# Two changes to a two-layer hybrid trunk step: all 16 K tiles of the heads' projection pairs by Strassen, and two of the rotation's six vector operations on GpSimd

## The chip, the core and the metric

The kernel runs on one core of a Trainium2 chip. The core has five engines with a queue of instructions each: TensorE (PE; its weight loads are listed as PEld), VectorE (DVE), ScalarE (ACT), GpSimd (POOL) and SyncE (SP). Each engine takes its queue in order; semaphores tie the queues together. The metric is the device time of one execution in microseconds (us), the median of the runs of a kernel.

## What is computed

The reference is one step of a two-layer trunk on 512 prompt tokens and 8 sample tokens, 520 columns in all, all in fp32. For each layer:

```python
h = rmsnorm(x)
B, C, xc, g_c, q, k, v, g_r = split(h @ w_in)          # 2048 x 8192
y_c = B * conv3(C * xc) * silu(g_c)                     # 1024 wide
q, k = rope(q), rope(k) / 16                            # 4 heads of 256
y_r = groupnorm(retention(q, k, v)) * silu(g_r)
x = x + concat(y_c, y_r) @ w_out
x = x + sigmoid(x @ w_pg) * (p @ w_ple)
```

`rope` takes the two halves `x1, x2` of a head's 256 rows and gives `x1*cos - x2*sin` and `x1*sin + x2*cos`. At the end stands a last norm. The outputs are the tokens and the new states of the convolution and the retention.

## The kernel before

**Layout.** Features lie on the 128 partitions and tokens on the free axis: 2048 features are 16 tiles of 128x520 (the K tiles), and a projection makes output tiles of 128x520. The tokens are worked in two halves of 260 columns, `LEFT` and `RIGHT`.

**Three matmuls for one product.** TensorE works on values rounded to fp32r, so every operand is split into a rounded part `hi` and a rest `lo`. A weight tile is split by `split_w` (line 225): ScalarE writes `hi` (line 229) and VectorE writes `lo` as the raw weights minus `hi` (line 230, two inputs from SBUF). A product of one weight tile (128x128) and one half of a K tile (128x260) is then three matmuls, lines 247, 248 and 249 (`mm3`).

**Pairs.** Output tiles are made in pairs. `plain` (line 270) makes all 2 x 16 x 2 = 64 products of a pair. `strassen` (line 290) takes the first `s` of the 16 K tiles as a 2x2 block scheme: two output tiles, even and odd K tiles, two halves of the tokens. There 7 products stand for 8, at the price of sums of weight tiles (`add`, line 315, VectorE at line 319, two SBUF inputs, four sums of `s/2` tiles a pair) and of sums of operand tiles that are built once for a stage. What is left of the K tiles behind `s` is done plainly in the same accumulators. The seven products of `s/2` tiles are cut by `times` (line 321) into chunks of at most 4 tiles; a chunk is one load into the split ring, one `split_w`, and 4 products, so 12 matmuls:

```python
        def times(out, raw, xs, start, more):
            for i, j in chunks(0, q, CHS):
                w = split_w(raw[:, P * i : P * j])
                product(out, w, 0, xs[i:j], start and i == 0, j == q, more)
                split_ring.put(*w)
```

With `s = 14`, `s/2 = 7`: each of the seven products is a chunk of 3 and a chunk of 4 tiles, and the two K tiles left over make two chunks of 2 tiles (`parts`, line 239), each used for 4 products. With `s = 16` every chunk has 4 tiles and nothing is left over. A pair with `s < 16` holds a fourth accumulator `c` and copies it once more on ScalarE (line 307 by way of `copy`, line 327, written `ps_g<-ps_g` in the profile).

**How many K tiles go by Strassen** stands in tables at the top: `HEADS` (line 53) for the 16 pairs of the four heads in each layer, `CONVS` (line 54) for the 16 pairs of the convolution's branch, and two more for `w_out` and `w_pg`. 0 means `plain`. In `CONVS` 13 of 16 entries are 16. The first two pairs of layer 0 are made apart, before the tables are used.

**The buffers that run ahead.** Raw weights come by SP's queue into a ring of 32 tiles (line 211). Split weights stand in a ring of 60 tiles (line 212): a chunk of 4 takes 8 of them, `hi` and `lo`, and gives them back when its last matmul is done. So ScalarE and VectorE can be up to seven chunks ahead of TensorE, and a wait of `split L229` or `split L230` for a matmul means that this ring is full.

**The heads' stage.** For each head `retain` (line 818) makes the pairs q, k, v and gate. q and k go through `rope` (line 749), six operations of 128x520 on VectorE, lines 753 to 758; `rc` and `rs` are the cosine and sine tables. The results go to memory by GpSimd's DMA queue (line 815, `hs`), and a head's retention is worked in nine later steps that lie between the products of the next pairs. Beside that run the 8 sample tokens' states: loads by GpSimd's queue (lines 771 and 772), VectorE at lines 781 and 785, and a store by GpSimd's queue (line 782). GpSimd itself computes only tiny powers (lines 633, 984, 1383) and fills small tiles; else it issues DMAs.

**What sets the order.** The order of the instructions of each engine is set at build time by a scheduler that estimates when each would be ready; weight splits and weight sums are raised in priority (lines 227 and 318). At run time each engine then follows that order.

Of the kernel before, what the change touches and what calls it, by code (L numbers as in the profile page):

```python
# [11 lines left out]
MUL, ADD, SUB = ALU.mult, ALU.add, ALU.subtract  # L12
# [37 lines left out]
EARLY = 6  # L50


HEADS = [[0, 0, 0, 8] + [14] * 12, [0] + [14] * 15]
CONVS = [[14] * 2 + [16] * 13 + [14]] * 2
OUT_ROWS = [[0, 8, 16, 16, 16, 16, 16, 0]] * 2

# [23 lines left out]
class Slots:  # L80
# [8 lines left out]
    def get(self, dtype=F32):  # L89
        i = self.free.pop(0)  # L90
        self.count += 1
        t = self.pool.tile([P, T], dtype, tag=f"s{i}", name=f"slot{i}_{self.count}")
        self.used[id(t)] = (t, i)
        return t
# [4 lines left out]
    def put(self, *slots):  # L99
        for t in slots:  # L100
            self.free.append(self.used.pop(id(t))[1])
# [90 lines left out]
def trunk_kernel(  # L192
# [6 lines left out]
    V, S, G, PE, DMA = nc.vector, nc.scalar, nc.gpsimd, nc.tensor, nc.sync  # L199
# [363 lines left out]
    def norm_g(l, k):  # L563
        return vec[:, 16 * l + k : 16 * l + k + 1]
# [97 lines left out]
    def from_dram(src):  # L662
        def load(k):
            t = get()
            SIDE.dma_start(t, src[k])
            return t

        return load

    xs = []  # L670
    X = Operands(HEADS[0][2:] + CONVS[0], from_dram(xT), gain=lambda k: norm_g(0, k))
    X.todo = [t for t in ((i, False, True) for i in range(max(X.rows) // 2))]
# [43 lines left out]
    for l in range(DEPTH):  # L716
# [5 lines left out]
        def prepare():  # L722
            rc, rs = get(), get()
            SIDE.dma_start(rc, cosT)
            SIDE.dma_start(rs, sinT)
            with tc.high_priority():
                root = rms.root()
                rb = rms.spread(rms.diagonal(root))
                V.tensor_tensor(rc, rc, rb, MUL)
                V.tensor_tensor(rs, rs, rb, MUL)  # L730
            return root, rb, rc, rs

        def copied(ps):
            t = get()
            for n, v in zip((LEFT, RIGHT), ps):
                S.activation(t[:, n], v, AF.Copy)
            banks.put(*[v for v in ps if not any(v is o for o in over)])
            return Val(put, slot=t)
# [3 lines left out]
        root, rb, rc, rs = prepare()  # L742
# [6 lines left out]
        def rope(z0, z1):  # L749

            a, b = ((z if z.ps is None else copied(z.ps)).slot for z in (z0, z1))
            t1, t2 = get(), get()
            V.tensor_tensor(t1, a, rc, MUL)
            V.tensor_tensor(t2, a, rs, MUL)
            V.tensor_tensor(a, b, rs, MUL)
            V.tensor_tensor(t1, t1, a, SUB)  # L756
            V.tensor_tensor(b, b, rc, MUL)
            V.tensor_tensor(b, b, t2, ADD)
            put(a, t2)
            return [t1, b]  # L760

# [56 lines left out]
        def retain(h):  # L818
# [6 lines left out]
            if l == 0 and h == 0:  # L825
                q = rope(*first[:2])
            else:
                q = rope(*head(mt))
# [5 lines left out]
            if l == 0 and h == 0:  # L834
                kf = rope(*first[2:])
            else:
                kf = rope(*head(mt + 2))
# [335 lines left out]
        if not tail:  # L1173
            X = Operands(HEADS[l + 1] + CONVS[l + 1], next_in, RESERVE_NEXT, gain=lambda k, l=l: norm_g(l + 1, k))
        for m in range(0, KT - tail, 2):
# [303 lines left out]
```

## Time and profile before

| | |
|---|---|
| runs of the kernel before | 2172.50, 2166.74, 2170.08 us; median 2170.08 us |
| profiled execution, own time | 2172.46 us |
| its span in the trace | 2170.4 us |
| busy in the span: PE, PEld | 2148.5, 2142.9 us |
| busy: DVE, ACT, POOL | 1895.7, 1266.2, 430.5 us |
| instructions | 48198, of them 17861 on PE |
| DMA | 387.31 MB, mean 178 GB/s |
| granted TensorE clock, mean | 0.998 |

The profiled execution's own time is 2.4 us above the median of the runs and about equal to the slowest of them. The heads' stages lie at about 60 to 400 us (layer 0) and 1105 to 1460 us (layer 1) of the span, the convolution's at about 400 to 745 and 1460 to 1815 us. A windows view gives the busy time of each engine in such a stretch; a timeline view lists instructions by start and duration; a waits view says who waited for whom, in us in total, times, and the longest; a lines view groups instructions by line and shape with the mean duration in ns of one.

### The profile page before, as it was taken

The page shows a single profiled execution, that of the slowest core. Times are in us where ns is not written, and L with a number is a line of the kernel's source. Part 1 is how long each engine was busy: PE and PEld are TensorE (multiplying, and loading weights), DVE is VectorE, ACT ScalarE, POOL GpSimd, SP SyncE. Part 2 cuts the span into 40 slices and gives each one's busy share as a digit, 9 for nine tenths or more (in the row PEclk, how much of TensorE's full clock was granted, in tenths as well). Part 3 has the DMA queues.
Part 4 walks back from the last instruction along what each step waited for, and adds up shares of the span by engine and source line. Part 5 has one row for each costly group of instructions (what it writes and reads, how often), then busy time and mean ns, then how long its engine had stood idle before and what let it go on. Part 6 is the DMA issues. An engine that isn't in the chain of part 4 may idle for free. (4 is left out here: it accounts for less than half of the span.)

```text
span 2170.4 us, 48198 instructions
## 1 busy us (share of the span) xinstructions
PE 2148.5 (99%) x17861; PEld 2142.9 (99%) x17861; DVE 1895.7 (87%) x3849; ACT 1266.2 (58%) x2661; POOL 430.5 (20%) x746
## 2 busy tenths in 40 slices
PE   9999999999999999999999999999999999999998
PEld 9999999999999999999999999999999999999998
DVE  8889989898999987987897988989999998878884
ACT  8656556655555555655765655565655555456565
POOL 2313222211001211210212222231111022121011
PEclk9999999999999999999999999999999999999999
DMA  8556675545543645645645566665464455566455
GB/s 288 176 169 196 185 215 183 186 152 172 156 134 120 228 156 186 217 153 161 214 144 174 172 210 193 190 195 183 147 182 145 127 155 199 181 212 195 127 169 192
DMA packets 182861, 387.31 MB, mean 178 GB/s; under 512 B 25888, under 2 KB 56352, under 8 KB 182624
## 3 DMA queue, kind: packets, MB, share of 16 engines
q1 hardware_dynamic: 129136, 213.77, 31.8%
q0 software_dynamic: 53056, 169.84, 23.8%
q8 instruction: 140, 2.29, 0.4%
q14 instruction: 97, 0.79, 0.1%
q10 hardware_dynamic: 432, 0.61, 0.1%
HBM read 318.96 MB, written 65.15 MB: 177 GB/s over the span
## 5 line engine op out<-in xcount | busy, mean ns | idle before, releaser
L247 PE MATMUL ps_g<-slot,split 128*128 128x260 f32 x5465 | 1532.3, 284 | 9.7 <-ACT slot L307 3.4
L248 PE MATMUL ps_g<-slot,split 128*128 128x260 f32 x5465 | 1535.1, 283 | 0.3 <-DVE slot L555 0.3
L249 PE MATMUL ps_g<-slot,split 128*128 128x260 f32 x5461 | 1520.5, 283 | 0.5 <-DVE split L230 0.5
L229 ACT ACTIVATE split<-raw 128x512 fp32r<-128x512 f32 (+2 forms) x1347 | 778.2, 596 | 587.6 <-DVE raw L319 205.6
L247 PEld LDWEIGHTS ps_g<-slot,split 128*128 128x128 f32 x5465 | 1024.5, 188 | 12.9 <-ACT slot L307 4.2
L248 PEld LDWEIGHTS ps_g<-slot,split 128*128 128x128 f32 x5465 | 1029.3, 188 | 0.5 <-DVE slot L555 0.5
L249 PEld LDWEIGHTS ps_g<-slot,split 128*128 128x128 f32 x5461 | 1020.3, 188 | 0.8 <-DVE split L230 0.7
L230 DVE TENSOR_TENSOR split<-raw,split 128x512 fp32r<-128x512 f32 (+2 forms) x1346 | 844.1, 647 | 176.5 <-PE ps_g L248 85.4
L319 DVE TENSOR_TENSOR raw<-raw 128x512 f32<-128x512 f32 (+1 forms) x660 | 426.2, 656 | 28.1 <-DMA raw<-wi 18.4
L307 ACT ACTIVATE slot<-ps_g 128x260 f32<-128x260 f32 x336 | 127.2, 381 | 142.5 <-PE ps_g L249 127.2
L551 ACT ACTIVATE slot<-slot 128x520 fp32r<-128x520 f32 (+1 forms) x212 | 109.1, 562 | 41.8 <-DVE slot L414 10.2
L552 DVE TENSOR_TENSOR slot<-slot,slot 128x520 fp32r<-128x520 f32 (+1 forms) x212 | 122.9, 609 | 4.3 <-ACT slot L551 4.2
L782 POOL DMA_DIRECT2D o_rets<-slot x64 | 35.3, 552 | 350.6 <-DVE slot L781 131.8
L307 DVE TENSOR_TENSOR slot<-ps_g,slot 128x260 f32<-128x260 f32 x168 | 70.5, 421 | 7.3 <-PE ps_g L249 4.9
L870 POOL DMA_DIRECT2D slot<-hs x64 | 46.1, 723 | 126.5 <-DVE split L230 35.5
L815 POOL DMA_DIRECT2D hs<-slot x64 | 35.6, 556 | 137.9 <-DVE slot L756 59.6
L747 DVE TENSOR_TENSOR slot<-slot,slot 128x520 f32<-128x520 f32 x80 | 55.4, 692 | 4.6 <-DMA o_rets<-slot 3.7
L1059 POOL DMA_DIRECT2D slot<-x1s x76 | 40.8, 538 | 88.0 <-PE ps_g L249 28.3
L781 DVE SCALAR_TENSOR_TENSOR slot<-slot,vs,slot 128x256 f32<-128x256 f32 x128 | 55.9, 477 | 2.6 <-ACT slot L777 2.3
L1209 POOL DMA_DIRECT2D x2s<-slot x30 | 16.3, 545 | 203.4 <-DVE slot L1204 202.5
L771 POOL DMA_DIRECT2D slot<-sret x64 | 35.5, 555 | 106.4 <-ACT split L229 43.4
L772 POOL DMA_DIRECT2D slot<-kq x64 | 34.9, 547 | 109.2 <-DVE slot L877 20.5
(217 smaller groups left out, 1727.0 us busy)
## 6 DMA issues: line engine op xcount, KB each, us to landing
raw<-wi SPq DMA_DIRECT2D x377, 256.0 KB, 3.9
raw<-wo SPq DMA_DIRECT2D x128, 256.0 KB, 5.6
raw<-wg SPq DMA_DIRECT2D x122, 256.0 KB, 4.2
raw<-wi SPq DMA_DIRECT2D x136, 192.0 KB, 4.0
slot<-x1s POOLq DMA_DIRECT2D x76, 260.0 KB, 5.0
slot<-sret POOLq DMA_DIRECT2D x64, 256.0 KB, 4.0
hs<-slot POOLq DMA_DIRECT2D x64, 256.0 KB, 3.9
slot<-hs POOLq DMA_DIRECT2D x64, 256.0 KB, 5.1
```

Of the source, the lines that this page charges most:

```text
L229: S.activation(hi, raw, AF.Copy)
L230: V.tensor_tensor(lo, raw, F(hi), SUB)
L247: PE.matmul(out, wh, xh, start=start, stop=False, skip_group_check=more)
L248: PE.matmul(out, wh, xl, start=False, stop=False, skip_group_check=more)
L249: PE.matmul(out, wl, xh, start=False, stop=stop, skip_group_check=more)
L307: fn(*args)
L319: V.tensor_tensor(out[:, n], x[:, n], y[:, n], op)
L551: keep(S.activation(hi, src[:, n], AF.Copy))
L552: V.tensor_tensor(lo, src[:, n], F(hi), SUB)
L747: V.tensor_tensor(out[:, n], v, table[:, n], MUL)
L781: keep(V.scalar_tensor_tensor(st[:, c], k, vs[:, h, e, b : b + 1], st[:, c], MUL, ADD))
L870: SIDE.dma_start(t[:, :512].rearrange("p (m n) -> p m n", m=2), src)
```

## The change

Two edits. In `HEADS`, the entries 14 become 16: 12 pairs in layer 0 and 15 in layer 1, 27 in all. The host packs these pairs' weights in the matching order of K tiles by the same table. In `rope`, the product `b * rs` (line 755) and the last sum (line 758) go from VectorE to GpSimd, and the product `b * rc` is written right behind the first of them.

```diff
-HEADS = [[0, 0, 0, 8] + [14] * 12, [0] + [14] * 15]
+HEADS = [[0, 0, 0, 8] + [16] * 12, [0] + [16] * 15]
...
             t1, t2 = get(), get()
             V.tensor_tensor(t1, a, rc, MUL)
             V.tensor_tensor(t2, a, rs, MUL)
-            V.tensor_tensor(a, b, rs, MUL)
+            G.tensor_tensor(a, b, rs, MUL)
+            V.tensor_tensor(b, b, rc, MUL)
             V.tensor_tensor(t1, t1, a, SUB)
-            V.tensor_tensor(b, b, rc, MUL)
-            V.tensor_tensor(b, b, t2, ADD)
+            G.tensor_tensor(b, b, t2, ADD)
             put(a, t2)
             return [t1, b]
```

Line 755 reads `b` and line 756 now overwrites it, so VectorE's line 756 waits for GpSimd's line 755; line 757 needs its result too; and GpSimd's line 755 overwrites `a`, so it waits for VectorE's lines 753 and 754.

SyncE's queue of weight loads shows the first edit. Before, in the heads' stage of layer 0 (`raw` is the ring of raw weights, `wi` the packed `w_in`; 128 columns are one tile):

```order
L312 DMA raw<-wi 128x512
L312 DMA raw<-wi 128x384
L312 DMA raw<-wi 128x512
L312 DMA raw<-wi 128x384
L312 DMA raw<-wi 128x512
L222 DMA raw<-wi 128x256 x2
L312 DMA raw<-wi 128x384
L312 DMA raw<-wi 128x512
L312 DMA raw<-wi 128x384 x2
```

And in the changed kernel, the end of the first stretch of layer 0 and all 12 changed pairs behind it:

```order
L222 DMA raw<-wi 128x512 x9
L312 DMA raw<-wi 128x512 x4
L222 DMA raw<-wi 128x512 x4
L312 DMA raw<-wi 128x512 x96
L312 DMA raw<-wi 128x384 x2
```

The chunks of 3 and 2 tiles are gone there: 12 pairs have 8 loads of 4 tiles each, 96 in a row, and the loads of 3 tiles begin again with the convolution's first pairs.

VectorE's queue at the second head's queries in layer 0, before (`slot_143_1422` is `a`, `slot_144_1423` is `b`, `slot_163_1701` and `slot_164_1702` are `t1` and `t2`, `slot_69_733` and `slot_70_734` the tables):

```order
L755 TENSOR_TENSOR slot_143_1422<-slot_144_1423,slot_70_734 128x520
L230 TENSOR_TENSOR split<-raw,split 128x512
L785 ISA slot_140_1403,osum<-slot_139_1402,slot_140_1403 128x256
L785 ISA osum 128x1
L230 TENSOR_TENSOR split<-raw,split 128x384
L756 TENSOR_TENSOR slot_163_1701<-slot_163_1701,slot_143_1422 128x520
L757 TENSOR_TENSOR slot_144_1423<-slot_144_1423,slot_69_733 128x520
L230 TENSOR_TENSOR split<-raw,split 128x512
L230 TENSOR_TENSOR split<-raw,split 128x256 x2
L758 TENSOR_TENSOR slot_144_1423<-slot_144_1423,slot_164_1702 128x520
```

The same place in the changed kernel (`a` is `slot_151_1441`, `b` is `slot_152_1442`, `t1` and `t2` are `slot_163_1690` and `slot_164_1691`):

```order
L754 TENSOR_TENSOR slot_164_1691<-slot_151_1441,slot_70_734 128x520
L230 TENSOR_TENSOR split<-raw,split 128x512 x3
L785 ISA slot_148_1423,osum<-slot_147_1422,slot_148_1423 128x256
L785 ISA osum 128x1
L230 TENSOR_TENSOR split<-raw,split 128x512
L756 TENSOR_TENSOR slot_152_1442<-slot_152_1442,slot_69_733 128x520
L757 TENSOR_TENSOR slot_163_1690<-slot_163_1690,slot_151_1441 128x520
```

Four splits and one sample operation stand between the last reader of `a` on VectorE (line 754) and line 756, which waits for GpSimd. GpSimd's queue there, in the changed kernel:

```order
L782 DMA o_rets<-slot_147_1422 128x512
L755 TENSOR_TENSOR slot_151_1441<-slot_152_1442,slot_70_734 128x520
L758 TENSOR_TENSOR slot_152_1442<-slot_152_1442,slot_164_1691 128x520
L815 DMA hs<-slot_163_1690 128x512
L815 DMA hs<-slot_152_1442 128x512
L771 DMA slot_174_1915<-sret 128x512
L772 DMA slot_175_1916<-kq 128x512
```

The two operations stand ahead of both `hs` stores and of the next sample's loads. Before, GpSimd's queue had only DMAs in that stretch:

```order
L782 DMA o_rets<-slot_139_1402 128x512
L815 DMA hs<-slot_163_1701 128x512
L771 DMA slot_174_1911<-sret 128x512
L815 DMA hs<-slot_144_1423 128x512
L772 DMA slot_175_1912<-kq 128x512
```

There the first `hs` store (of `t1`) could leave when VectorE's line 756 was done; now both stores wait behind line 758.

## Prediction

> **What bounds the kernel now.** I read the page's first part, then who TensorE waits for, then the stages one by one. The page:
>
> ```profile
> PE 2148.5 (99%) x17861; PEld 2142.9 (99%) x17861; DVE 1895.7 (87%) x3849; ACT 1266.2 (58%) x2661; POOL 430.5 (20%) x746
> ```
>
> TensorE is busy for all but 22 us of the span. A busy PE is not proof of a limit, so I looked at its waits in the waits view. These are the longest three in total; the columns are us, times, longest:
>
> ```profile
> PE ps_g L247 <- ACT slot L307: 3.4, 4, 1.1
> PE ps_g L247 <- ACT ps_g L307: 2.9, 4, 1.1
> PE ps_g L247 <- ACT split L229: 1.9, 1, 1.9
> ```
>
> Next to nothing: TensorE runs through. Now the busy times by stage: the heads' two stages, the convolution's two stages, and two quieter stretches inside the latter. Columns are the stretch, its length, then PE, PEld, DVE, ACT, POOL busy (x instructions), clock, DMA share, GB/s:
>
> ```profile
> 60.00:400.00 340.00, 339.97 (x2837) 339.28 (x2836) 306.05 (x672) 202.46 (x442) 94.04 (x163) 1.00 0.59 188
> 400.00:745.00 345.00, 340.30 (x2822) 339.51 (x2821) 315.92 (x636) 195.88 (x421) 55.80 (x88) 1.00 0.52 161
> 1105.00:1460.00 355.00, 353.00 (x2940) 351.52 (x2939) 311.79 (x682) 206.65 (x461) 90.58 (x154) 1.00 0.58 181
> 1460.00:1815.00 355.00, 352.34 (x2938) 351.38 (x2938) 329.62 (x667) 202.82 (x433) 57.35 (x92) 1.00 0.53 166
> ...
> 500.00:600.00 100.00, 100.00 (x837) 100.00 (x836) 89.93 (x177) 52.76 (x108) 13.19 (x23) 1.00 0.53 161
> 1500.00:1600.00 100.00, 100.00 (x840) 100.00 (x839) 93.06 (x186) 57.72 (x119) 17.76 (x30) 1.00 0.55 169
> ```
>
> The heads lose 0.03 and 2.00 us of TensorE. At full load 837 matmuls take 100 us, 119.5 ns each. VectorE is second: 90% and 88% in the heads. The convolution, most of whose pairs have all 16 K tiles by Strassen already, holds 93.06% of VectorE for 100 us with TensorE full. That is what the heads are to become.
>
> How much VectorE may fall behind is told by the waits on the split ring, first in 60 to 400 us, then in 1105 to 1460 us:
>
> ```profile
> ACT split L229 <- PE ps_g L248: 20.6, 32, 2.2
> ACT split L229 <- PE ps_g L249: 20.5, 36, 1.8
> ...
> ACT split L229 <- PE ps_g L248: 25.4, 34, 2.0
> ACT split L229 <- PE ps_g L249: 13.5, 12, 2.4
> ```
>
> 114 times in 695 us the splitting waits because the ring is full. A chunk of 4 tiles feeds 12 matmuls, 12 x 119.5 ns = 1.43 us, and the ring holds seven, so a full ring is up to 10 us of work in hand. A stall of VectorE of one or two us does not reach TensorE there.
>
> **The change part by part.** *TensorE.* Of a pair, 14 tiles by Strassen are 7 x 7 products and the two left-over tiles 4 x 2, together 57; 16 tiles are 7 x 8 = 56. One product is 3 matmuls, 27 pairs, so 81 matmuls go, all 128x260: 81 x 119.5 ns = **-9.7 us**, all on the path, since TensorE never stops.
>
> *VectorE.* The rows by line and shape (columns: busy us, mean ns of one | idle before it):
>
> ```profile
> L230 DVE TENSOR_TENSOR split<-raw,split 128x512 fp32r<-128x512 f32 x1031 | 690.9, 685 | 152.9 <-PE ps_g L248 81.9 <-ACT split L229 53.8 <-issue 7.2
> L319 DVE TENSOR_TENSOR raw<-raw 128x512 f32<-128x512 f32 x520 | 351.9, 684 | 13.7 <-DMA raw<-wi 6.6 <-DMA raw<-wo 4.6
> L230 DVE TENSOR_TENSOR split<-raw,split 128x384 fp32r<-128x384 f32 x249 | 136.1, 550 | 15.3 <-ACT split L229 8.0 <-PE ps_g L248 3.6 <-ACT slot L551 1.6
> L319 DVE TENSOR_TENSOR raw<-raw 128x384 f32<-128x384 f32 x140 | 76.9, 550 | 14.4 <-DMA raw<-wi 11.8 <-DMA raw<-wg 2.1
> L230 DVE TENSOR_TENSOR split<-raw,split 128x256 fp32r<-128x256 f32 x66 | 27.0, 417 | 8.3 <-ACT split L229 8.1
> L755 DVE TENSOR_TENSOR slot<-slot,slot 128x520 f32<-128x520 f32 x16 | 11.1, 691 | 0.0
> ```
>
> Seven splits a pair grow from 3 to 4 tiles, 189 x (685 - 550) = +25.5 us; two splits of 2 tiles go, 54 x 417 = -22.5 us. Four sums a pair grow by a tile, 108 x (684 - 550) = +14.5 us. The rotation gives up lines 755 and 758, which is as long: 32 x 691 = -22.1 us. Together -4.6 us: the second edit pays for the first. ScalarE has the same splits and 27 copies fewer; at 58% it bounds nothing. The DMAs move the same bytes in fewer, larger loads.
>
> *GpSimd.* 32 operations of 128x520 with two inputs from SBUF. The trace has none of that size. Its rows for fills and for the smallest power with two inputs:
>
> ```profile
> L596 POOL MEMSET half_neg<- 128x32 f32 x1 | 0.1, 121 | 0.0
> L885 POOL MEMSET slot<- 128x128 f32 x8 | 1.8, 225 | 0.0
> L984 POOL TENSOR_TENSOR rstp<-rstd,half_neg 128x2 f32<-128x2 f32 x16 | 14.4, 900 | 20.1 <-DVE rstd L983 20.1
> ```
>
> 96 elements more cost 104 ns, 1.08 ns an element for one stream. 520 elements are 0.1 + 0.56 = 0.7 us if the two inputs and the output flow together, and 0.1 + 3 x 0.56 = 1.8 us one after another. I take 1.2 us, two streams in turn, an estimate from these rows. GpSimd is 20% busy, so its own time matters little. What matters is VectorE beside it. Timelines of both engines at three of GpSimd's powers (columns: start us, duration us):
>
> ```profile
> 673.00 0.69 DVE L319 TENSOR_TENSOR raw<-raw 128x512 f32<-128x512 f32 x1
> 674.76 0.69 DVE L230 TENSOR_TENSOR split<-raw,split 128x512 fp32r<-128x512 f32 x1 [1.07 <-issue]
> ...
> 673.17 5.83 POOL L1383 TENSOR_TENSOR rsn<-va,half_neg 128x32 f32<-128x32 f32 x1 [15.82 <-DVE va L1381]
> ...
> 1434.26 0.68 DVE L319 TENSOR_TENSOR raw<-raw 128x512 f32<-128x512 f32 x1
> 1434.86 0.55 DVE L230 TENSOR_TENSOR split<-raw,split 128x384 fp32r<-128x384 f32 x1
> ...
> 1434.50 1.49 POOL L984 TENSOR_TENSOR rstp<-rstd,half_neg 128x2 f32<-128x2 f32 x1 [1.74 <-DVE rstd L983]
> ...
> 358.39 0.68 DVE L319 TENSOR_TENSOR raw<-raw 128x512 f32<-128x512 f32 x1
> ...
> 358.46 1.19 POOL L984 TENSOR_TENSOR rstp<-rstd,half_neg 128x2 f32<-128x2 f32 x1
> ```
>
> At 673 us VectorE stands still for 1.07 us with nothing in the profile that it waits for, while GpSimd reads. At 1434 and 358 us VectorE runs on and GpSimd's 2-element power, 0.90 us on average, takes 1.49 and 1.19 us. So an operation of each engine with two SBUF inputs holds off the other. A held-off VectorE loses between 0 and 1.8 us per GpSimd operation; I take the whole 1.2 us, since line 756 waits for line 755 anyway. 32 x 1.2 = 38.4 us. The Trainium skill, page "SBUF — State Buffer", section "Who interferes with whom", says that such a pair contend for one read interface, and that whoever starts first holds it for its whole instruction. The trace agrees that one blocks the other; that the block lasts the whole instruction it does not show, 1.07 us of 5.83. By the rule the term stays as I took it; by 1.07 us as the most, it would be 32 x 1.07 = 34.2 us and the share below 94.5%.
>
> VectorE in the heads is then 306.05 + 311.79 - 4.6 + 38.4 = 651.6 us of 695 - 9.7 = 685.3 us, **95.1%**, a little over the 93.06% that a stretch of the convolution holds with TensorE full. Here I choose: 1460 to 1815 us, at 92.9%, lost 2.66 us of TensorE in 355, most of it where the stage ends. Doubled to 685 us that is 5.1, against 2.0 now; half of the difference I give to the heads, **+1.5 us**, bounds -2.0 (today's waits go) and +20 (below).
>
> *The new waits.* VectorE's line 756 waits for GpSimd's 755; behind it stand the splits of the next chunks. GpSimd's queue must be free then. It mostly is: it waits for VectorE at the rotation's stores already, here in layer 1:
>
> ```profile
> POOL hs L815 <- DVE slot L756: 39.8, 8, 17.2
> ```
>
> In the changed order at least two, at 14 of the 16 rotations four or more operations of VectorE stand between lines 754 and 756, so the wait costs it little beyond the blocking already counted. The full ring covers it; without that cover it would be 16 times up to 1.2 us, 19 us. The stores of q and k leave a few us later; they are read again a pair or more later.
>
> The sum: 2172.46 us (the profiled execution) - 9.7 + 1.5 = 2164.3; against the median, 2170.08 - 8.2 = **2161.9 us**.
>
> **The rivals.** *A: the blocking eats half of the gain.* Suppose that VectorE can't be used beyond 95% of the heads, 651 us, before TensorE waits one for one. If a GpSimd operation takes from VectorE as long as the two held-up powers took, (1.49 + 1.19) / 2 = 1.34 us, VectorE's load without blocking, 617.84 - 4.6 = 613.2 us, becomes 613.2 + 32 x 1.34 = 656.1 us, 5.1 us over: -9.7 + 5.1 = -4.6, 2165.5 us, no change that can be told. For it: the 1.07 us block. Against: the ring is full 114 times. The Trainium skill, page "GPSIMD Engine Reference", section 3.1, has GpSimd about 1.96 times slower than VectorE at adding two tensors, which on 691 ns would be an estimate of 1.35 us. No run here shows it yet.
>
> *B: VectorE becomes the bound, slower.* Same mechanism, at the upper bound of 1.8 us: 613.2 + 57.6 = 670.8, 20 us over, -9.7 + 20 = +10, 2180 us. It turns to a loss from (651 + 9.7 - 613.2) / 32 = 1.48 us per operation. For it: at 1434 us each engine held the other off in turn, so that both may lose. Against: VectorE's idle time in the heads, 77 us now, would still not be used up (670.8 of 685).
>
> *C: GpSimd costs VectorE nothing,* as at 358 us, where its operation ran its usual 0.68 us. Then VectorE stays at 613.2 of 685 us, 89.5%, as today, and today's 2.0 us of waits may go too: -11.7, 2158.4 us. Against: the 1.07 us.
>
> **How the numbers follow.** My forecast gets 0.47, C 0.13, A 0.25, B 0.15. About 0.3% (6.5 us) is what a measurement of this kernel can tell from no change. Faster by more is the forecast and C, 0.60; the same is A, 0.25; slower is B, 0.15. The range from 2158 to 2172 us holds the forecast, A and nearly all of C, and leaves out B and the rest.
>
> **What would show it.** Right: 81 matmuls fewer at the same 119.5 ns, TensorE's busy time down by about 9.7 us; lines 755 and 758 on POOL near 1.2 us each; VectorE's waits for POOL at line 756 some us in all; DVE near 95% of the heads' stages counting blocked time. Wrong: TensorE idle by more than some 5 us in the heads, waiting for splits (lines 229 and 230), with GpSimd's operations just before, or GpSimd's operations at 1.8 us and more; then B. A median under 2158 would say C.

## The result, and the profile after

| | before | after |
|---|---|---|
| median of the runs beside each other | 2168.77 us (4 runs) | 2191.09 us (4 runs) |
| profiled execution: span | 2170.4 us | 2184.8 us |

The ratio is 1.0099 [1.0075, 1.0123]: slower by about 22 us where 8 us faster was forecast. The profiled execution of the changed kernel (2186.6 us) is the quickest of its runs, so its trace shows the smaller part of the loss, 14.4 us between the spans.

The page of the changed kernel:

```profile
span 2184.8 us, 47686 instructions
PE 2151.3 (98%) x17780; PEld 2141.4 (98%) x17780; DVE 1924.3 (88%) x3763; ACT 1260.5 (58%) x2580; POOL 497.7 (23%) x778
```

The 81 matmuls are gone, but TensorE's busy time rose by 2.8 us. Idle it was 2170.4 - 2148.5 = 21.9 us before and is 2184.8 - 2151.3 = 33.5 us now. The two heads' stages, in the columns of the windows shown before:

```profile
60.00:400.00 340.00, 331.76 (x2709) 329.04 (x2708) 310.40 (x613) 193.01 (x394) 125.73 (x176) 0.98 0.56 183
...
1105.00:1460.00 355.00, 346.14 (x2843) 343.17 (x2842) 321.98 (x629) 198.12 (x405) 122.99 (x166) 0.99 0.55 177
```

In the same stretches TensorE gets through 128 and 97 matmuls fewer than before, and it idles 17 us of 695 where it idled 2. Whom it waits for (us, times, longest):

```profile
PE ps_g L247 <- ACT slot L307: 13.3, 11, 3.1
PE ps_g L247 <- ACT split L229: 4.8, 5, 1.8
PE ps_g L247 <- ACT ps_g L307: 1.7, 1, 1.7
PE ps_g L249 <- DVE split L230: 1.5, 4, 0.6
```

ScalarE is named in all the long ones, with 58% of its time in use. What ScalarE itself waits for is seen in one of them. The timeline of the changed kernel from 344 to 353 us, GpSimd, VectorE, ScalarE and TensorE in turn (start us, duration us, in brackets the idle time before and its releaser):

```profile
344.80 3.23 POOL L755 TENSOR_TENSOR slot<-slot,slot 128x520 f32<-128x520 f32 x1 [0.78 <-DVE slot L754]
349.88 1.66 POOL L758 TENSOR_TENSOR slot<-slot,slot 128x520 f32<-128x520 f32 x1 [0.98 <-DVE slot L756]
...
346.79 2.38 DVE L230 TENSOR_TENSOR split<-raw,split 128x512 fp32r<-128x512 f32 x2
349.10 0.69 DVE L756 TENSOR_TENSOR slot<-slot,slot 128x520 f32<-128x520 f32 x1
349.71 0.69 DVE L757 TENSOR_TENSOR slot<-slot,slot 128x520 f32<-128x520 f32 x1
350.32 1.50 DVE L785 CUSTOM_DVE_ANT_0 slot<-slot,slot 128x256 f32<-128x256 f32 x1
...
350.43 0.21 ACT L839 ACTIVATE qks<-slot 128x8 f32<-128x8 f32 x1 [1.29 <-DVE slot L757]
351.91 0.94 ACT L307 ACTIVATE slot<-ps_g 128x260 f32<-128x260 f32 x3 [1.27 <-DVE osum L785]
...
352.35 0.59 PE L247 MATMUL ps_g<-slot,split 128*128 128x260 f32 x1 [3.02 <-ACT slot L307]
```

Read it upwards. TensorE stands for 3.02 us until ScalarE has copied an accumulator (line 307). ScalarE is late because line 839, ahead of that copy in its queue, waits 1.29 us for VectorE's line 757, and the copy itself 1.27 us more until VectorE's line 785 is through. VectorE never pauses, but twice it is held off: the two splits at 346.79 take 2.38 us instead of some 1.3, and line 785 takes 1.50 us instead of the 0.41 us that it has elsewhere, each while GpSimd's line 755 or 758 runs. Splits are not what is missing: ScalarE's splits at 345.05 and 346.50 us had themselves waited for a matmul, so the ring of split weights was full shortly before.

After such a wait TensorE is slow for a while longer. Windows of the changed kernel, from just ahead of the wait to behind it, and two more (third column on: PE busy and matmuls; the seventh is the granted clock):

```profile
351.40:358.20 6.80, 5.85 (x27) 5.85 (x28) 5.38 (x12) 3.14 (x8) 4.33 (x9) 0.50 0.71 240
358.20:361.60 3.40, 3.40 (x30) 3.40 (x30) 3.40 (x9) 0.47 (x1) 0.00 (x0) 0.99 0.00 0
252.40:255.80 3.40, 3.40 (x16) 3.19 (x15) 3.40 (x11) 0.13 (x1) 2.67 (x5) 0.51 1.02 277
1327.60:1331.00 3.40, 3.40 (x18) 3.40 (x18) 3.40 (x10) 0.29 (x2) 2.54 (x6) 0.51 0.90 266
1430.00:1433.40 3.40, 3.40 (x18) 3.40 (x17) 3.10 (x8) 1.55 (x3) 2.12 (x4) 0.51 0.71 267
```

At half the clock 16 to 18 matmuls pass in 3.4 us instead of 30. In the four stretches 27 + 16 + 18 + 18 = 79 matmuls keep TensorE busy for 5.85 + 3 x 3.4 = 16.05 us; at 119.5 ns they need 9.4, so 6.6 us are lost. The heads of the kernel before have no such stretch, both their windows show 1.00; that kernel has one in the convolution's stage, behind a wait of 1.95 us (16 matmuls from 729.4 to 732.8 us, 1.5 us lost). The Trainium skill, page "TensorE: Matmul & The Clock Gate", section "Why this matters for your kernels", warns of gaps above about 3 us; here a gap of 3.02 us is followed by the half clock, but so is one of 1.76 us at 250 us, so by these runs the limit is lower than stated or depends on where the gap falls.

The spans add up: -9.7 us of matmuls, +11.6 us of idle time, and +12.5 us inside the busy time (2.8 + 9.7), of which the half clock behind waits is 6.6 - 1.5 = 5.1 and the rest is not told apart here; together +14.4.

### The profile page after: what moved, and what is told of

It is laid out like the page before. It is cut to its first block, busy times and chain, and to the rows that moved or that the text cites. A ratio compares the mean times of both kernels' runs of the same rounds, so it can differ in the third digit from the quotient of the medians.

```text
span 2184.8 us, 47686 instructions
## 1 busy us (share of the span) xinstructions
PE 2151.3 (98%) x17780; PEld 2141.4 (98%) x17780; DVE 1924.3 (88%) x3763; ACT 1260.5 (58%) x2580; POOL 497.7 (23%) x778
## 5 line engine op out<-in xcount | busy, mean ns | idle before, releaser
L247 PE MATMUL ps_g<-slot,split 128*128 128x260 f32 x5434 | 1528.1, 284 | 21.7 <-ACT slot L307 13.3
L229 ACT ACTIVATE split<-raw 128x512 fp32r<-128x512 f32 (+1 forms) x1292 | 779.6, 620 | 592.1 <-DVE raw L319 244.0
L230 DVE TENSOR_TENSOR split<-raw,split 128x512 fp32r<-128x512 f32 (+1 forms) x1292 | 865.9, 688 | 182.2 <-PE ps_g L248 96.2
L319 DVE TENSOR_TENSOR raw<-raw 128x512 f32<-128x512 f32 (+1 forms) x660 | 442.5, 680 | 23.6 <-DMA raw<-wi 17.9
L1141 POOL DMA_DIRECT2D x1s<-slot x32 | 17.4, 545 | 186.6 <-DVE slot L1139 186.6
L785 DVE CUSTOM_DVE_ANT_0 slot<-slot,slot 128x256 f32<-128x256 f32 x128 | 57.2, 447 | 0.0
```

The costliest lines, as they stand in the source:

```text
L229: S.activation(hi, raw, AF.Copy)
L230: V.tensor_tensor(lo, raw, F(hi), SUB)
L247: PE.matmul(out, wh, xh, start=start, stop=False, skip_group_check=more)
L319: V.tensor_tensor(out[:, n], x[:, n], y[:, n], op)
L785: V.tensor_tensor_reduce(k, st[:, c], kb[:, :256], 1.0, 0.0, MUL, ADD, osum[:, e, h, b : b + 1])
```

## The experiments

Three theories stood first. **S**: ScalarE's queue stops at the small copies of queries and keys (lines 830 and 839), which wait for GpSimd's line 758. **V**: VectorE, held off by GpSimd's reads, is too late by itself. **K**: VectorE's own work in the heads is already too much with all 16 tiles. Each run is compared with runs of the kernel before on the same chip, whose median lay between 2168.6 and 2171.1 us.

**Each edit alone.** The first with the table only:

```diff
-HEADS = [[0, 0, 0, 8] + [14] * 12, [0] + [14] * 15]
+HEADS = [[0, 0, 0, 8] + [16] * 12, [0] + [16] * 15]
```

> The first edit alone: 27 pairs with 16 K tiles by Strassen, the rotation as before, all six operations on VectorE. Theory S (ScalarE's queue: its copies for the sample tokens wait for GpSimd's line 758, and the weight splits and accumulator copies behind them come late) and theory V (VectorE held off by GpSimd's reads, 32 x 1.17 us, runs short by itself) both say that the loss comes with GpSimd: 81 x 119.5 ns = 9.7 us less than before plus some 2 us of new waits, 2159 to 2163 us, ratio to before 0.996 to 0.998. Theory K (the sixteenth tile itself overloads VectorE: +17.5 us there in the heads with nothing given back, 92.7% busy) says slower than before, 2175 us and more.

Measured: 2182.63 us, 1.0061 [1.0047, 1.0074], as K expected. The second with 14 tiles and the changed rotation:

```diff
-            V.tensor_tensor(a, b, rs, MUL)
-            V.tensor_tensor(t1, t1, a, SUB)
+            G.tensor_tensor(a, b, rs, MUL)
             V.tensor_tensor(b, b, rc, MUL)
-            V.tensor_tensor(b, b, t2, ADD)
+            V.tensor_tensor(t1, t1, a, SUB)
+            G.tensor_tensor(b, b, t2, ADD)
```

> The second edit alone: 14 K tiles as before, lines 755 and 758 on GpSimd. Theories S and V: the same stalls as in the changed kernel without its 9.7 us of matmuls saved, 2190 to 2200 us, with TensorE waiting for ScalarE's lines 229 and 307 in the heads and its clock granted at half after the longest of these. Theory K: VectorE is relieved of 22 us and pays 37 us for blocking; near before, 2165 to 2175 us.

Measured: 2190.52 us, 1.0100 [1.0087, 1.0113], as S and V expected. Each edit loses by itself, +14 and +22 us, and both together lose +22: they don't add. The heads of the run with 16 tiles alone:

```profile
60.00:400.00 340.00, 331.18 (x2735) 329.00 (x2734) 307.12 (x635) 191.87 (x396) 93.67 (x161) 0.99 0.58 184
...
1105.00:1460.00 355.00, 346.36 (x2876) 343.89 (x2875) 320.77 (x651) 198.15 (x406) 90.29 (x150) 1.00 0.56 178
```

VectorE is busy 90.3% of the time there, less than the 93.06% that the prediction thought safe, and TensorE idles 17.5 us.

**ScalarE freed of the small copies.** The changed kernel with:

```diff
-                S.activation(qks[:, d, :NS], q[d][:, SEQ:T], AF.Copy)
+                G.tensor_copy(qks[:, d, :NS], q[d][:, SEQ:T])
...
-                S.activation(qks[:, 2 + d, :NS], kf[d][:, SEQ:T], AF.Copy)
+                G.tensor_copy(qks[:, 2 + d, :NS], kf[d][:, SEQ:T])
```

> The changed kernel, but the copies of the sample tokens' eight columns of q and k (lines 830 and 839) go from ScalarE to GpSimd, behind line 758 in its own queue, so ScalarE never waits for the rotation. GpSimd's two operations a rotation and their blocking of VectorE stay. Theory S: most of the loss goes, 2160 to 2172 us. Theory V: it stays, 2183 to 2193 us.

Measured: 2189.03 us, 1.0101 [1.0087, 1.0115], no better than the changed kernel. S falls. In the changed kernel ScalarE waited 21.5 us in the heads at these small copies, and in this one not at all; yet TensorE's waits for ScalarE's copies of line 307 stay (12.8 us against 13.3) and those for its splits grow (10.7 us against 4.8).

**GpSimd's reads with nobody waiting for them.** 16 tiles; the rotation is four VectorE operations (the products of line 755 and the sum of line 758 are left out of the results), and GpSimd makes the two operations into a tile that nobody reads:

```diff
             V.tensor_tensor(t2, a, rs, MUL)
-            V.tensor_tensor(a, b, rs, MUL)
-            V.tensor_tensor(t1, t1, a, SUB)
+            G.tensor_tensor(aside_out, t2, rs, MUL)
             V.tensor_tensor(b, b, rc, MUL)
-            V.tensor_tensor(b, b, t2, ADD)
+            V.tensor_tensor(t1, t1, t2, SUB)
+            G.tensor_tensor(aside_out, t1, rs, ADD)
```

> Sixteen K tiles; four operations of the rotation on VectorE as in the changed kernel, and two GpSimd operations of the same size at the same places, whose result goes to a tile that nothing reads. The rotated q and k leave out the terms with b*sin and a*sin in the right places, so the outputs are not the reference's. Blocking of VectorE as in the changed kernel, 32 x 1.1 to 1.2 us; no instruction of VectorE or ScalarE waits for GpSimd's result. Theory V: as slow as the changed kernel, 2183 to 2193 us. Theory S: 2158 to 2166 us.

Measured: 2209.99 us, 1.0189 [1.0176, 1.0202], slower than either theory had it. Then the same without GpSimd's two operations, at 16 and at 14 tiles:

> All 16 tiles by Strassen, and the rotation cut to four VectorE operations (left out: the products of line 755 and the sum of line 758, so the keys and queries are wrong); nothing of it on GpSimd. Against the run with all 16 tiles alone VectorE does 32 x 0.69 = 22 us less in the heads. K (bursts of VectorE's work in the heads starve TensorE, and the longer splits and sums tip it): TensorE's idle time in the heads falls from 20 us to under 6, and the 81 matmuls show: 2157 to 2164 us, ratio 0.995 to 0.998. O (it is not VectorE's work but the 16-tile schedule itself, its chunks and loads): the loss stays, 2176 to 2183 us, ratio 1.003 to 1.006.

> 14 tiles as in the kernel before, and the rotation cut to the same four VectorE operations (left out: lines 755 and 758's work). The kernel before idles TensorE only 2.8 us in the heads, so a lighter VectorE can give no more than that. K: 2165 to 2169 us, ratio 0.998 to 1.000, so that 16 tiles beat 14 by 4 to 10 us once the rotation is light. O: the same time here, but 14 tiles stay 10 us and more ahead of 16.

Measured: 2171.96 us, 1.0004 [0.9993, 1.0014] with 16 tiles; 2172.52 us, 1.0007 [0.9998, 1.0017] with 14. The first lies between the ranges of K and O, the second above both: with 14 tiles a lighter rotation gains nothing. So 32 operations of GpSimd for whose results nobody waits cost some 40 us: 41.4 over the kernel before with them, 0.9 without. The wait of line 756 is not what hurts. And a third thing is seen: this kernel with 16 tiles has on VectorE what the forecast's changed kernel had if GpSimd were free (rival C, 2158.4 us), and it is no faster than before.

**Writes in the place of reads.** 16 tiles and the light rotation, with two fills at each place of an operation:

```diff
+            G.memset(a, 0.0)
+            G.memset(a, 0.0)
             V.tensor_tensor(b, b, rc, MUL)
             V.tensor_tensor(t1, t1, t2, SUB)
+            G.memset(t2, 0.0)
+            G.memset(t2, 0.0)
```

> 16 tiles, the light rotation, and on GpSimd two fills of 128x520 at each place where the changed kernel has an operation (on tiles whose values are no longer needed; about 0.66 us each by the rows for fills, so as long as the operation, and written, not read). R (GpSimd costs VectorE time by reading two inputs while VectorE reads two): fills cost nothing, within 4 us of the light rotation at 16 tiles, and VectorE's operations beside them keep their 0.68 us. P (any GpSimd operation in SBUF holds VectorE off): 64 x about 0.6 us more on VectorE, 2195 to 2210 us, as with the reads that nobody waits for.

Measured: 2174.44 us, 1.0015 [1.0001, 1.0029], 2.5 us above the same without fills. One line of busy times from the page of each, first the light rotation, then with fills, then with reads:

```profile
PE 2142.0 (99%) x17780; PEld 2133.0 (98%) x17780; DVE 1898.1 (88%) x3763; ACT 1258.9 (58%) x2580; POOL 430.3 (20%) x746
```

```profile
PE 2141.8 (99%) x17780; PEld 2134.2 (98%) x17780; DVE 1898.6 (88%) x3763; ACT 1259.2 (58%) x2580; POOL 464.2 (21%) x810
```

```profile
PE 2155.4 (98%) x17780; PEld 2142.1 (97%) x17780; DVE 1930.2 (87%) x3763; ACT 1258.4 (57%) x2580; POOL 514.4 (23%) x778
```

VectorE does the same 3763 instructions in all three. 34 us of fills on GpSimd add 0.5 us to them, 84 us of reads 32.1 us: the reading holds VectorE off, the writing does not (R). The Trainium skill says so in "SBUF — State Buffer", section "Who interferes with whom": a VectorE operation with two SBUF inputs contends with a GpSimd one that reads SBUF, not with one that only writes. The runs agree. How much of the 40 us comes by this way is not told apart: GpSimd's queue, which issues the stores and loads of the heads too, is also held 84 us longer by the reads and only 34 us by the fills.

**Only the quiet pairs by 16.** Why 16 tiles alone cost 14 us was open. 15 of the 27 pairs, with the rotation as before:

```diff
+HEADS = [[0, 0, 0, 8] + [16, 14, 14, 16] * 3, [0] + [16] * 3 + [16, 14, 14, 16] * 3]
```

> The rotation as in the kernel before, and all 16 tiles in 15 of the 27 pairs: queries and gates of heads 1 to 3 of both layers, and keys, values and gates of head 0 of layer 1; 45 matmuls fewer, 45 x 119.5 ns = 5.4 us. K (the loss stands where the longer splits meet the rotations, the samples and the retention's steps): fewer places overflow, 2163 to 2171 us, ratio 0.997 to 1.001. O (each 16-tile pair costs its share, 13 + 9.7 us over 27 pairs): 2176 us, ratio 1.003.

Measured: 2185.00 us, 1.0062 [1.0047, 1.0078], outside what either theory expected. 15 pairs cost as much as 27. A fourth theory was **Z**: it is not the work but the order that the scheduler gives it.

**The same work in another order.** In the kernel before, and in the one with 16 tiles alone:

```diff
-            V.tensor_tensor(t1, t1, a, SUB)
             V.tensor_tensor(b, b, rc, MUL)
+            V.tensor_tensor(t1, t1, a, SUB)
```

> The kernel before with lines 756 and 757 written in the other order: the same instructions, the same buffers, 14 tiles, nothing on GpSimd. The scheduler then gives another order to 1431 of VectorE's 3273 rows. Z (the loss is the order: the kernel before has a favourable one, and any other order of this crowded stage costs, whatever the work): slower by 4 to 14 us, 2174 to 2184 us, ratio 1.002 to 1.006, with new idle time of TensorE in the heads. K (VectorE's amount of work in the heads): nothing changes, 2168 to 2173 us, ratio 0.999 to 1.001.

> All 16 tiles, the rotation on VectorE with the same two lines swapped: the same work as the run with 16 tiles alone (2182.6 us) in another order. Z: another time, off by more than 4 us to one side or the other (2165 to 2179, or over 2186). K: the same time, 2180 to 2185 us.

Then 16 tiles alone with `SPLIT = 64`, and with `MORE_HEAD = 2`:

> All 16 tiles, the rotation on VectorE, and the ring of split weights 64 tiles instead of 60, so that eight whole chunks of 4 tiles fit instead of seven and a half. If the lead over TensorE is what is short in the heads (bursts of VectorE's work), one chunk more, 1.43 us of work in hand, takes idles of up to 1.4 us away: 2165 to 2175 us. Z: another order again, anything from 2165 to 2190 us, with the idle time at other places.

> All 16 tiles, the rotation on VectorE, and up to two operand sums built at a time where the heads' stage builds one (MORE_HEAD 2): the same work, the sums earlier. Z: another order, another time than 2182.6 us by more than 4 us. K: the same or worse, 2180 to 2190 us, since the sums bunch.

Measured: the swap costs the kernel before 4 us, 2173.47, 1.0018 [1.0009, 1.0027], between the ranges of K and Z. The three kernels with 16 tiles came to 2186.68, 1.0074 [1.0060, 1.0088]; 2185.46, 1.0074 [1.0060, 1.0088]; and 2182.25, 1.0053 [1.0038, 1.0068]. Against 2182.63 that is within about 4 us. The order is worth up to 4 us either way; 16 tiles lose in every one of four orders. Z is too small to explain it, and one more chunk of lead does not help.

**VectorE's work by itself.** To test K alone, the kernel before, with 14 tiles and nothing on GpSimd, got two useless VectorE operations more in each rotation, or one (only the first of the two):

```diff
             V.tensor_tensor(a, b, rs, MUL)
+            V.tensor_tensor(aside_out, t2, rs, MUL)
             V.tensor_tensor(t1, t1, a, SUB)
             V.tensor_tensor(b, b, rc, MUL)
+            V.tensor_tensor(aside_out, t1, rs, ADD)
             V.tensor_tensor(b, b, t2, ADD)
```

> 14 tiles, nothing on GpSimd, the rotation of the kernel before and two further VectorE operations of 128x520 in each into a tile that nobody reads: 32 x 0.69 = 22 us more on VectorE, slack 52 us. K: as much lost as at that slack with 16 tiles alone and with the quiet pairs, 17 to 24 us, 2186 to 2194 us, ratio 1.008 to 1.011. O: VectorE has room for it, within 5 us of the kernel before.

> The same with one further VectorE operation in each rotation: 11 us more, slack 63 us. K: half as much, 8 to 16 us lost, 2177 to 2186 us. O: within 3 us of the kernel before.

Measured: 2189.14 us, 1.0086 [1.0070, 1.0103] with two; 2183.40 us, 1.0061 [1.0046, 1.0076] with one, both as K expected. By the count 11 us of VectorE work (8.7 us more busy time in the trace) cost 14 us of time, though VectorE had 75 us to spare on average. The longest wait of TensorE in the run with one, VectorE first, then TensorE (line numbers are up to two higher than in the kernel before):

```profile
1245.61 0.70 DVE L755 TENSOR_TENSOR slot<-slot,slot 128x520 f32<-128x520 f32 x1 [2.31 <-DMA o_rets<-slot]
...
1247.31 0.69 DVE L757 TENSOR_TENSOR aside_out<-slot,slot 128x520 f32<-128x520 f32 x1
...
1249.55 0.69 DVE L230 TENSOR_TENSOR split<-raw,split 128x512 fp32r<-128x512 f32 x1
...
1250.29 0.39 PE L249 MATMUL ps_g<-slot,split 128*128 128x260 f32 x1 [3.13 <-DVE split L230]
```

VectorE first stands 2.31 us until a sample's store has read a buffer that the rotation wants to write. Then eight entries run without a pause, the useless one (line 757) among them, before the split that TensorE stands 3.13 us for; ScalarE had written its half of that split by 1245.56 us. Another way is seen in the run with two, from 1334 us on: VectorE, then ScalarE, then TensorE (line numbers here are up to three higher than in the kernel before):

```profile
1335.71 0.69 DVE L758 TENSOR_TENSOR slot<-slot,slot 128x520 f32<-128x520 f32 x1
1336.32 0.69 DVE L759 TENSOR_TENSOR slot<-slot,slot 128x520 f32<-128x520 f32 x1
...
1339.36 0.68 DVE L760 TENSOR_TENSOR aside_out<-slot,slot 128x520 f32<-128x520 f32 x1
1339.96 0.69 DVE L761 TENSOR_TENSOR slot<-slot,slot 128x520 f32<-128x520 f32 x1
...
1343.08 0.12 DVE L986 TENSOR_SCALAR rstd<-mv 128x2 f32<-128x2 f32 x1
1345.41 0.43 DVE L230 TENSOR_TENSOR split<-raw,split 128x256 fp32r<-128x256 f32 x1 [2.22 <-ACT split L229]
...
1340.68 0.21 ACT L842 ACTIVATE qks<-slot 128x8 f32<-128x8 f32 x1 [1.25 <-DVE slot L761]
1344.96 0.42 ACT L229 ACTIVATE split<-raw 128x256 fp32r<-128x256 f32 x1 [4.08 <-DMA raw<-wi]
...
1345.43 0.58 PE L247 MATMUL ps_g<-slot,split 128*128 128x260 f32 x1 [5.45 <-ACT split L229]
```

From 1326 to 1343 us VectorE has no gap: a rotation, the state of a sample, steps of the retention, and the splits and sums between them. The splits come late, ScalarE then waits 4.08 us for raw weights, and TensorE stands 5.45 us. The load was late in part because of VectorE: from 1332 to 1339 us SyncE's queue waits 6.5 us for VectorE, 3.1 of them for one split (line 230) to free the raw ring. The load then leaves at 1338.79 us and takes 6.2 us to land, where line 222's loads take 3.7 us in the median.

The useless operations stand inside the rotation, so these two runs do not separate VectorE's amount of work from the lateness of what stands behind the rotation.

**Still less on VectorE, with 16 tiles.** The rotation keeps only `a*rc` and `b*rc`:

> All 16 tiles, and of the rotation only two VectorE operations (left out: lines 754, 755, 757 and 758 or their like, so queries and keys are wrong): 64 x 0.69 = 44 us less on VectorE than with 16 tiles alone. Slack below is the time that TensorE's matmuls need in the heads less the time that VectorE's work takes there: 692 - 618 = 74 us in the kernel before, 47 with 16 tiles alone, 70 with the light rotation, 91 here. K (time is lost as soon as VectorE's slack in the heads falls below what the kernel before has): nothing is lost and the 81 matmuls show, 2159 to 2163 us, ratio 0.995 to 0.997. O (16 tiles cost 10 us by themselves, whatever VectorE does): as with the light rotation, 2168 to 2173 us.

Measured: 2168.06 us, 0.9995 [0.9984, 1.0005]. Less work brings more back, but at the edge of O's range and not in K's: of the 9.7 us some 8 stay lost.

**Room for VectorE in a kernel whose outputs stay right.** 16 tiles alone, with `CHA = 8` instead of 4, so that a sum of weight tiles is one operation of 128x1024:

> All 16 tiles, the rotation on VectorE, and the sums of weight tiles made in one operation of 128x1024 instead of two of 128x512, in the whole kernel (CHA 8; the outputs stay right). By the rows of 128x512 and 128x384 one operation has about 0.15 us that don't grow with its size; 4 fewer a pair are 0.6 us, 16 us over 27 pairs of the heads, slack 63 us. K: a part of the loss comes back, 2172 to 2180 us. O: the loss stays, 2180 to 2186 us.

Measured: 2204.17 us, 1.0161 [1.0143, 1.0180], far worse. VectorE's busy time in the heads fell from 627.9 to 615.6 us, and TensorE's idle time there rose from 17.5 to 21.4. Less work did not help, so K by the amount alone fails here; that a split which is wanted at once now stands behind a longer sum is the likely reason, but was not tested.

All runs in one table. Slack is 693 us (TensorE's busy time in the heads before, 339.97 + 353.00; the expectations take 692) less VectorE's 618, changed by the counts of the prediction and of the expectations, 0.69 us for a line of the rotation, and 38 us for GpSimd's reads; lost is the time over the kernel before, plus 119.5 ns for every matmul saved.

| kernel | tiles | slack us | lost us |
|---|---|---|---|
| light rotation | 14 | 97 | 1 |
| before | 14 | 75 | 0 |
| before, two lines swapped | 14 | 75 | 4 |
| one operation more | 14 | 64 | 14 |
| GpSimd alone | 14 | 59 | 22 |
| two operations more | 14 | 53 | 20 |
| rotation of two | 16 | 92 | 8 |
| light rotation | 16 | 70 | 11 |
| light rotation, fills | 16 | 70 | 13 |
| whole sums | 16 | 64 | 44 |
| quiet pairs | 15 of 27 | 60 | 19 |
| 16 tiles alone | 16 | 48 | 24 |
| the same, lines swapped | 16 | 48 | 27 |
| the same, ring of 64 | 16 | 48 | 26 |
| the same, two sums at a time | 16 | 48 | 23 |
| both (the change) | 16 | 32 | 32 |
| both, small copies on GpSimd | 16 | 32 | 30 |
| unwaited reads | 16 | 32 | 51 |

Less slack mostly goes with more loss, but it does not set it: at 64 us one kernel loses 14 us and another 44.

No version here beats the kernel before by more than its measurement can tell.

## Why the prediction was wrong

**The step that failed** is the one that judged VectorE's load by a share: 95.1% in the heads, "a little over the 93.06% that a stretch of the convolution holds with TensorE full", with 1.5 us given for it. In place of these 1.5 us the changed kernel's trace has 17.1 - 2.0 = 15 us more idle time of TensorE in the heads and 6.6 us at half clock, and this with VectorE at 91.0% there (632.4 of 695 us), not at 95.1%. Two runs show it with neither edit in them: at (618 + 11) / 693 = 91% the loss is 14 us, at 92.4% 20 us. With 14 tiles the heads' limit is just above the 89% that they have in the kernel before. The comparison was also with the better of the convolution's two stages: by the prediction's own table the other, at 91.6%, lost 4.70 us of TensorE in 345.

Why the convolution holds 93% where the heads do not is not shown, and no run adds work to the convolution. Stretches in which VectorE is full are not the difference. Windows of 10 us of the kernel before, two in the heads and two in the convolution (DVE is the third busy time):

```profile
1180.00:1190.00 10.00, 10.00 (x87) 10.00 (x86) 5.59 (x11) 3.08 (x7) 0.00 (x0) 1.00 0.65 244
1200.00:1210.00 10.00, 10.00 (x86) 10.00 (x86) 10.00 (x23) 5.34 (x13) 1.98 (x4) 1.00 0.82 243
...
1570.00:1580.00 10.00, 10.00 (x86) 10.00 (x85) 9.83 (x19) 6.75 (x16) 0.56 (x1) 1.00 0.52 145
1610.00:1620.00 10.00, 10.00 (x85) 10.00 (x85) 10.00 (x22) 6.89 (x15) 1.64 (x3) 1.00 0.48 143
```

Over both stages VectorE is busy for all 10.00 us in 16 of 69 windows of the heads (60 to 400 and 1110 to 1460 us) and in 14 of 69 of the convolution (400 to 740 and 1460 to 1810 us). The heads only fall lower: 10 windows under 7.5 us, against 1. What the traces do show is the way from VectorE to TensorE: at the three long waits shown above, an entry in the queue of ScalarE, of SyncE or of VectorE itself stands late, and what TensorE needs stands behind it.

**"A full ring ... a stall of one or two us does not reach TensorE there"** fell with it. The ring being full often says nothing of it: in the heads ScalarE's splits wait for a matmul 80.0 us in the kernel before and 83.6 us in the run with one useless operation, which loses 14 us. In the 3.02 us wait above TensorE wanted an accumulator that ScalarE copied late, with the ring full shortly before. ScalarE at 58% "bounds nothing" only as long as no entry of its queue waits for VectorE.

**The -9.7 us** were counted rightly, 17780 matmuls, but "all on the path, since TensorE never stops" was true of before only. Of the 14-tile kernel's 57 products, those of the two left-over tiles need splits but no sums; with them goes work that TensorE could do while VectorE caught up. That this is why 16 tiles still lose some 8 us with the lightest rotation is argued; which part of the stage takes those 8 us stays open.

**VectorE's own sum, -4.6 us,** came out 7 us too low. The light rotation with 16 tiles does the VectorE work that the sum counts, and VectorE is busy 1898.1 us in it against 1895.7 before, +2.4 us. The table alone costs 19.8 us (1915.5) where 17.5 were counted, and 32 operations of the rotation give back 17.4 where 22.1 were: operations in a row overlap, as lines 756 and 757 above, 0.69 us long and 0.61 apart.

**GpSimd's price, 38.4 us,** was somewhat too high. The changed kernel has the same 3763 VectorE instructions as the light rotation with 16 tiles; VectorE is busy 1924.3 - 1898.1 = 26.2 us longer, and it waited for line 755:

```profile
DVE slot L756 <- POOL slot L755: 4.8, 4, 1.2
```

26.2 + 4.8 = 31.0 us, 0.97 us for an operation and not 1.2. That the wait at line 756 costs little was right too; the operations around it that are held off are the price. GpSimd's operation takes 1.29 us at the least, near the 1.2 taken, but the bound of 1.8 us was too low:

```profile
L755 POOL TENSOR_TENSOR slot<-slot,slot 128x520 f32<-128x520 f32 x16 | 37.9, 2372 | 41.3 <-DVE slot L754 25.1 <-ACT slot L307 16.1
L758 POOL TENSOR_TENSOR slot<-slot,slot 128x520 f32<-128x520 f32 x16 | 28.5, 1784 | 16.3 <-DVE slot L756 16.2
```

**The rivals.** B named the right sign and engine, but put its turning point at 1.48 us per operation, by the same 95%. With the limit near 90% it is passed at much less: the loss came at 0.97 us. Its argument from 1434 us misread the rows, where VectorE's two operations have their usual 0.68 and 0.55 us and only GpSimd's is longer. None of the rivals had a clock that halves after a wait: 6.6 us in the trace, against 1.5 in the kernel before and a whole forecast gain of 8.2.

**What stays open:** why the heads have less room than the convolution; those 8 us; why whole sums, which take work from VectorE, lose 20 us more; why reads that nobody waits for lose 51 us where the changed kernel at the same slack loses 32; and why 15 pairs cost nearly what 27 do.

## What to carry to other kernels

An engine's share of busy time over a stage is no measure of the room it has, and a share that another stage holds is no limit for this one. Nor do shorter windows tell the two stages apart here. A stage that shows almost no waits may be at its edge; the cheapest test is to add a little useless work to the suspected engine in the kernel as it is, which here showed 14 us lost for 11 us of work. Then follow the longest new wait back through the queues. Moving a two-input operation to GpSimd relieves VectorE of 0.69 us at the most and holds it off for about 1.0 in this kernel, so it pays only where VectorE has gaps; 64 fills on GpSimd added 0.5 us to VectorE's time.

## What the hardware showed beside this

**GpSimd and VectorE hold each other off.** GpSimd's 128x520 operation of two inputs takes 1.3 us at the least and up to 4.04 us in the changed kernel. Two of them in the changed kernel, the first with the VectorE operation that stood aside, the second behind five VectorE operations in a row:

```profile
241.95 1.30 POOL L755 TENSOR_TENSOR slot<-slot,slot 128x520 f32<-128x520 f32 x1 [3.09 <-DVE slot L754]
316.60 3.78 POOL L755 TENSOR_TENSOR slot<-slot,slot 128x520 f32<-128x520 f32 x1 [2.65 <-ACT slot L307]
...
242.11 1.43 DVE L785 CUSTOM_DVE_ANT_0 slot<-slot,slot 128x256 f32<-128x256 f32 x1
316.71 1.89 DVE L230 TENSOR_TENSOR split<-raw,split 128x512 fp32r<-128x512 f32 x3
318.52 0.68 DVE L319 TENSOR_TENSOR raw<-raw 128x512 f32<-128x512 f32 x1
320.41 0.70 DVE L756 TENSOR_TENSOR slot<-slot,slot 128x520 f32<-128x520 f32 x1 [1.21 <-POOL slot L755]
```

At 242 us GpSimd comes first, and VectorE's 0.41 us become 1.43: it ends 0.29 us after GpSimd's operation. At 316 us VectorE's operations follow each other and run at their usual 0.6 us each; GpSimd's is shown as running from 316.60, but ends only 3.78 us later, when VectorE had to wait for it.

**Half a clock after short waits.** Idle times of 1.76, 1.77, 3.02 and 3.06 us in the changed kernel's stream of matmuls each came with 3.4 or 6.8 us at a granted clock of 0.5, which began between 1 us before and 1.5 us after the matmuls resumed; two of 1.73 and 1.92 us, at 82 and 1384 us, did not, nor did one of 2.14 us at 310 us with 16 tiles alone.

**Longer operations of less work can cost.** With 16 tiles in the heads, one sum of 128x1024 (1.22 us) in place of two of 128x512 (0.68 us each) in the whole kernel made it some 20 us slower; the reason is not shown.
